# Issuing 72 spill stores from GpSimd's queue in place of SyncE's, in a two-layer hybrid backbone on one core

## The chip, the cores and the metric

The kernel runs on one core of a Trainium2 chip. The metric is the device time of one execution in microseconds; the median of three runs is taken. A core has four engines that compute (TensorE for matrix products, VectorE, ScalarE and GpSimd) and SyncE, which only issues transfers between the chip's main memory and the on-chip buffer. Each engine works through its own instructions in order, and an instruction that waits holds all that stand behind it on the same engine.

## What is computed

Two layers act on 512 latent tokens and 256 context tokens of width 1024. Each layer normalises its input, projects it to three groups of heads, and maps their gated outputs back:

```python
u = _modulate(h_lat, sh, sc) @ w_in[i]
y_hy = _hyena(u_hy, ...)                       # two long convolutions with implicit filters
xs, Bh, Ch, z_s, dt, a = _ssd_prep(u_ss, ...)
y_ss, _, _ = _ssd_bidir(xs, Bh, Ch, dt, a, s_f, s_b)   # chunked scan, both directions
y_ss = _ssd_finish(y_ss, xs, z_s, ...)         # gate and group norm
y_at = _window_attention(q, k, v, kc, vc, attn_sinks[i]) * jax.nn.silu(z_a)
out = jnp.concatenate([y_hy, y_ss, y_at], axis=-1) @ w_out[i]
new_lat = _layernorm(DEEPNORM_ALPHA * h_lat + g * out) * ln_g[i] + ln_b[i]
```

The context runs through the same weights; in the second layer only its keys, values and scan states are needed.

## The kernel before

Matrices stand in float32 and are split into a high and a low part, so that one product becomes three on TensorE. A projection (`proj`) loads a block of 128 x 1024 weights (L439), splits it (`split`, L178 on ScalarE and L179 on VectorE) and multiplies it with all tokens: 512 latent columns into the accumulator pl (two buffers, L461) and, where the context is needed, 256 columns into pc (one buffer, L463). The raw weight tile has two buffers, shared with the table loads of L202.

The on-chip buffer is too small for all that lies between the stages, so results are spilled to main memory and read back later. Five places store:

- `att` runs attention by blocks of 128 queries and stores each block's output (L686); the queries are read in through L611.
- `ssm` runs the scan by chunks of 128 tokens and stores each chunk's output (L863). Per chunk and group it loads a broadcast tile R (L844, three buffers) of row sums; VectorE and ScalarE add to it (L850, L852), and the product M of L857 is the last that reads it.
- `hy_in` projects the inputs of the long convolution, in steps V, 1, 2 and G, and stores each (L887 for V, L889 for the others). Step G reads step 2 back (L878).
- `gate_mul`, called by `ssm_gate` and `att_gate`, projects a gate, reads a spilled output back into U (L486), multiplies (L489) and stores it in place (L490). Its tile V has two buffers. Where the context is needed VectorE first clears the column between the sequences (L482), then forms the gate from the accumulators (L474).
- Other stores (of the filters, L349, of the long convolution's result, L991, and of the output) are not touched.

Between these, `modulation` loads weights through L365 and multiplies them (L370, then a copy L372 and L375); it is advanced one step at a time between projections. In the long convolution GpSimd takes one product of each frequency tile (L949), and in `ssm_gate` the power of the norm (L523).

All transfers are issued by SyncE before the change. Dependencies between tiles are tracked and turned into waits when the kernel is built, and a planner then lays out each engine's instructions; their order on an engine is not the order of the code. A load that reads a spilled tile back waits for the store to have landed, whichever queue issued it, and a buffer is reused only when the transfer that reads it has landed.

Of the kernel before, what the change touches and what calls it, by code (L numbers as in the profile page):

```python
# [18 lines left out]
P = 128  # L19
# [27 lines left out]
class Net:  # L47
# [428 lines left out]
    def gate_mul(self, l, b0, j, xt, sp, both):  # L476

        nc = self.nc
        n = WID if both else SEQ
        g = self.ip("V", [P, QW])  # L480
        if both:
            nc.vector.memset(g[:, SEQ:CO], 0.0)  # L482
        self.gate(*self.proj(l, b0 + j, xt, both), g)
        y = self.ip("U", [P, WID + 2])
        for c0, w in ((0, SEQ), (CO, CTX)) if both else ((0, SEQ),):
            nc.sync.dma_start(y[:, c0:c0 + w], sp[j, :, c0:c0 + w])  # L486
        if both:
            nc.vector.memset(y[:, SEQ:CO], 0.0)
        nc.vector.tensor_tensor(g[:, :n], y[:, :n], g[:, :n], op=ALU.mult)  # L489
        nc.sync.dma_start(sp[j, :, :n], g[:, :n])  # L490
        return g, y

    def att_gate(self, l, xt, sp, last):
# [97 lines left out]
    def att(self, l, q, ks, vt, last):  # L591

        nc = self.nc
        sp = self.dr.tile([4, P, QW], F32, name=self.nm("sp"))
        for n in list(range(4)) + ([] if last else [4, 5]):
            lat = n < 4
            q0 = n * P if lat else n * P + 1
# [67 lines left out]
            for hp in range(0, 4, 2):  # L665
                pts = []
                for i in range(nk):
# [4 lines left out]
                    t = self.w("pt", [P, 2, 256], bufs=5)  # L672
# [10 lines left out]
                        if i == 0:  # L683
                            self.after(m, turned)
            nc.scalar.activation(q[:, :, q0:q0 + P], pv.rearrange("p (h q) -> p h q", h=4), AF.Copy, scale=0.5)
            nc.sync.dma_start(sp[:, :, q0:q0 + P].rearrange("j p t -> p j t"), q[:, :, q0:q0 + P])  # L686
        return sp


# [90 lines left out]
    def ssm(self, l, xT, bt, bc, sc, rd, last):  # L780

        nc = self.nc
        sp = self.dr.tile([4, P, QW], F32, name=self.nm("sp"))
# [29 lines left out]
        for c in (0, 1, 2, 3) if last else (4, 5, 0, 1, 2, 3):  # L813
            q0 = col(c)
            pg = self.wk()
            for g in range(2):
                nc.tensor.matmul(pg[:, g * P:(g + 1) * P], lhsT=bc[:, g, q0:q0 + P], rhs=bc[:, 2 + g, q0:q0 + P], start=True, stop=True)
            gm = self.w("gm", [P, 2, P], bufs=2)
            nc.scalar.activation(gm, pg[:, 0:256].rearrange("p (g l) -> p g l", g=2), AF.Copy)

            own = self.ts([P, 10])
            for g in range(2):
                t = self.w("dg", [P, P])
                nc.vector.scalar_tensor_tensor(t, gm[:, g], 1.0, self.ident, op0=ALU.mult, op1=ALU.mult, accum_out=own[:, 8 + g:9 + g])
                w = slice(4 * g, 4 * g + 4)
                nc.vector.scalar_tensor_tensor(own[:, w], vec(DT, 1, c)[:, w], own[:, 8 + g:9 + g], dcol[:, w], op0=ALU.mult, op1=ALU.add)
            py = self.wk()
            ys = self.w("ys", [P, 512], bufs=3)
            nc.vector.tensor_tensor(h64(ys), h64(xT[:, c]), bc64(own[:, 0:8]), op=ALU.mult)
            for d in range(2):  # L830
                if states[d, c] is None:
                    continue
                po = self.wk()
                for g in range(2):
                    nc.tensor.matmul(po[:, 256 * g:256 * g + 256], lhsT=bc[:, 2 + g, q0:q0 + P], rhs=states[d, c][:, 256 * g:256 * g + 256], start=True, stop=True)
                yo = self.w("yo", [P, 512], bufs=3)
                nc.vector.tensor_tensor(h64(yo), h64(po), bc64(vec(EX, d, c)), op=ALU.mult)
                nc.vector.tensor_tensor(ys, ys, yo, op=ALU.add)
            for j in range(4):
                nc.tensor.matmul(py[:, j * P:(j + 1) * P], lhsT=ys[:, j * P:(j + 1) * P], rhs=self.ident, start=j == 0, stop=False, is_transpose=True, skip_group_check=True)  # L840

            for g in range(2):
                R = self.w("R", [P, 2, 4, P], bufs=3)
                nc.sync.dma_start(R, rd[:, 8 * c + 4 * g:8 * c + 4 * g + 4].partition_broadcast(P))  # L844
                for d in (1, 0):
                    for h in range(4):
                        hh = 4 * g + h
                        bias = vec(LB, d, c)[:, hh:hh + 1]
                        if h % 2 == 0 and d == 0:
                            nc.vector.tensor_scalar_add(R[:, d, h], R[:, d, h], bias)  # L850
                        else:
                            nc.scalar.activation(R[:, d, h], R[:, d, h], AF.Identity, bias=bias)  # L852
                E = R[:, 1]
                nc.vector.copy_predicated(E, self.upper.unsqueeze(1).to_broadcast([P, 4, P]), R[:, 0])
                nc.scalar.activation(E, E, AF.Exp)
                M = self.w("M", [P, 4, P], bufs=2)
                nc.vector.tensor_tensor(M, E, gm[:, g].unsqueeze(1).to_broadcast([P, 4, P]), op=ALU.mult)  # L857
                for h in range(4):
                    hh = 4 * g + h
                    r0, j = 64 * (hh % 2), hh // 2  # L860
                    nc.tensor.matmul(py[r0:r0 + 64, j * P:(j + 1) * P], lhsT=xT[:, c, 64 * hh:64 * hh + 64], rhs=M[:, h], start=False, stop=True, skip_group_check=True)
            nc.scalar.activation(bc[:, :, q0:q0 + P], py.rearrange("p (j l) -> p j l", j=4), AF.Copy, scale=0.5)
            nc.sync.dma_start(sp[:, :, q0:q0 + P].rearrange("j p t -> p j t"), bc[:, :, q0:q0 + P])  # L863
        return sp


    def hy_in(self, l, xt, last, b0, fill, x2s, sp, js=range(4)):
        nc = self.nc
        n = SEQ if last else WID
        for j in js:  # L870
            pl, pc = self.proj(l, b0 + j, xt, not last)
            t = self.ip("V", [P, QW])
            if b0 == B_GH:
                if not last:
                    nc.vector.memset(t[:, SEQ:CO], 0.0)
                self.gate(pl, pc, t)
                x2 = self.ip("U", [P, WID + 2])
                nc.sync.dma_start(x2[:, :n], x2s[j, :, :n])  # L878
                nc.vector.scalar_tensor_tensor(t[:, :n], t[:, :n], 0.5, x2[:, :n], op0=ALU.mult, op1=ALU.mult)
            else:  # L880
                i = C_HCW + 4 * ((b0 - B_HV) + j)
                self.conv(pl, pc, self.par[:, l, i:i + 4], t, False)
            if b0 == B_HV:

                f = self.ip("U", [P, WID + 2])
                for c0, L in ((0, SEQ),) if last else ((0, SEQ), (CO, CTX)):
                    nc.sync.dma_start(sp[j, :, c0:c0 + L], self.fold(t, f, c0, L))  # L887
            else:
                nc.sync.dma_start(sp[j, :, :n], t[:, :n])  # L889
            next(fill, None)  # L890

    def fold(self, v, f, c0, L):
# [476 lines left out]
```

## Time and profile before

| | us |
|---|---|
| median of 3 runs (1282.61 to 1287.61) | 1284.53 |
| the profiled execution | 1286.6 |
| its span, first to last instruction | 1284.8 |
| TensorE, busy in the span | 1212.7 |
| VectorE | 953.7 |
| ScalarE | 595.0 |
| GpSimd | 133.8 |

The transfers move 208.94 MB at a mean of 163 GB/s. TensorE's mean granted clock is 0.984 of full speed. A busy TensorE is not TensorE at its peak, since its products are pipelined and their ends are modelled; the idle time before an instruction, and what released it, say more. A wait for several things is put down to the one that came last.

### The profile page before, as it was taken

Reading aid. Unit: us, or ns where it says so; the run is one execution under the profiler, and the core shown is the slowest. Engines: PE = TensorE matmul, PEld = TensorE weight load, DVE = VectorE, ACT = ScalarE, POOL = GpSimd, SP = SyncE. Lnnn points to the kernel's source line nnn. Section 1 sums busy time; section 2 is a strip of 40 time slices with the busy share of each in tenths; the row PEclk is TensorE's granted clock in tenths of the full one; section 3 lists DMA queues with packets and bytes.
Section 4 is the critical chain, followed back from the end, with each engine's and each line's share of the span. In section 5 each row is a group of like instructions: output and inputs, shape, how many; then the busy total and the mean of one; then the engine's idle time right before and its main releaser. Section 6 shows DMA issues by size and latency. Waiting matters only on the chain.

```text
span 1284.8 us, 19311 instructions
## 1 busy us (share of the span) xinstructions
PE 1212.7 (94%) x6966; PEld 974.5 (76%) x6966; DVE 953.7 (74%) x1982; ACT 595.0 (46%) x1157; POOL 133.8 (10%) x117
## 2 busy tenths in 40 slices
PE   5988999999999999999999999999999999899997
PEld 3656788778776867799877777887877686788776
DVE  6986845987764885499746899777777588598676
ACT  5557623766434273333224454456644526343440
POOL 1421110000000000022110332100000000011102
PEclk9988999999999999999999999999999999999999
DMA  7775363321117477854488852431123725945872
GB/s 238 244 262 195 115 198 98 83 67 50 58 42 227 146 210 264 273 158 140 153 269 289 270 158 95 110 112 59 34 74 115 220 100 157 287 149 190 281 234 82
DMA packets 109192, 208.94 MB, mean 163 GB/s; under 512 B 10553, under 2 KB 55033, under 8 KB 109096
## 3 DMA queue, kind: packets, MB, share of 16 engines
q1 hardware_dynamic: 109096, 207.70, 51.3%
q8 instruction: 55, 0.90, 0.3%
q14 instruction: 41, 0.34, 0.1%
HBM read 162.44 MB, written 38.41 MB: 156 GB/s over the span
## 4 chain that ended last, share of the span: by engine, by line
PE 57%; DVE 14%; DMA 11%; issue 9%; ACT 4%; POOL 2%; SPq 1%; POOLq 0%; DVEq 0%; ACTq 0%
PE pl L461 19%; PE pc L463 7%; PE wk L183 4%; PE wk L184 4%; PE wk L185 4%; PE wk L682 3%; PE wk L671 3%; DMA R<-rd 2%; PE wk L633 2%; DVE wl L179 2%; PE wk L643 1%; PE wk L370 1%; DMA wo<-in_w_out_dram 1%; ACT wh L178 1%; DMA wr<-in_tab_dram 1%
## 5 line engine op out<-in xcount | busy, mean ns | idle before, releaser
L461 PE MATMUL pl<-Q,wh 128*128 128x512 f32 x1168 | 410.8, 403 | 0.9 <-ACT wh L178 0.5
L461 PEld LDWEIGHTS pl<-Q,wh 128*128 128x128 f32 x1168 | 218.1, 190 | 57.2 <-issue 8.1
L461 PE MATMUL pl<-Q,wl 128*128 128x512 f32 x584 | 233.0, 399 | 0.0
L463 PE MATMUL pc<-Q,wh 128*128 128x256 f32 x704 | 185.7, 291 | 6.0 <-DVE V L474 4.7
L178 ACT ACTIVATE wh<-wr 128x1024 fp32r<-128x1024 f32 x76 | 80.4, 1057 | 158.4 <-PE pc L463 76.8
L463 PEld LDWEIGHTS pc<-Q,wh 128*128 128x128 f32 x704 | 127.8, 191 | 13.7 <-DVE V L474 6.6
L461 PEld LDWEIGHTS pl<-Q,wl 128*128 128x128 f32 x584 | 110.8, 190 | 24.5 <-issue 1.2
L179 DVE TENSOR_TENSOR wl<-wr,wh 128x1024 fp32r<-128x1024 f32 x76 | 99.5, 1312 | 26.8 <-ACT wh L178 26.7
L949 POOL TENSOR_TENSOR ta<-ta 128x256 f32<-128x256 f32 x40 | 32.2, 804 | 712.3 <-DVE ta L947 687.0
L463 PE MATMUL pc<-Q,wl 128*128 128x256 f32 x352 | 101.7, 289 | 0.0
L463 PEld LDWEIGHTS pc<-Q,wl 128*128 128x128 f32 x352 | 67.2, 191 | 2.0 <-issue 1.4
L178 ACT ACTIVATE wh<-wo 128x1024 fp32r<-128x1024 f32 x30 | 31.6, 1058 | 47.0 <-DMA wo<-in_w_out_dram 27.1
L648 ACT ACTIVATE pr<-wk,S 128x512 f32<-128x512 f32 (+2 forms) x80 | 47.9, 604 | 11.5 <-DVE S L647 10.7
L852 ACT ACTIVATE R<-R,sc 128x128 f32<-128x128 f32 x120 | 38.4, 390 | 26.3 <-DMA R<-rd 26.3
L646 DVE TENSOR_REDUCE S<-wk 128x1 f32<-128x512 f32 (+2 forms) x80 | 45.0, 578 | 6.9 <-PE wk L644 4.1
L179 DVE TENSOR_TENSOR wl<-wo,wh 128x1024 fp32r<-128x1024 f32 x30 | 36.5, 1221 | 12.5 <-ACT wh L178 12.4
L671 PE MATMUL wk<-con,pr 128*128 128x128 f32 x320 | 45.4, 277 | 0.1
L183 PE MATMUL wk<-ph,Q 128*128 128x256 f32 x144 | 41.7, 298 | 2.8 <-ACT ph L178 2.7
L671 PEld LDWEIGHTS wk<-con,pr 128*128 128x128 f32 x320 | 36.1, 140 | 8.4 <-issue 4.4
L178 ACT ACTIVATE yh<-ta 128x512 fp32r<-128x512 f32 x32 | 20.2, 631 | 47.3 <-DVE ta L950 47.3
L184 PE MATMUL wk<-plo,Q 128*128 128x256 f32 x144 | 41.3, 291 | 0.3 <-DVE plo L179 0.3
L185 PE MATMUL wk<-ph,Q 128*128 128x256 f32 x144 | 40.6, 288 | 0.0
(404 smaller groups left out, 2901.1 us busy)
## 6 DMA issues: line engine op xcount, KB each, us to landing
wr<-in_w_in_dram SPq DMA_DIRECT2D x76, 512.0 KB, 4.3
Q<-in_w_mod_dram SPq DMA_DIRECT2D x24, 1024.0 KB, 8.0
wo<-in_w_out_dram SPq DMA_DIRECT2D x43, 512.0 KB, 5.0
kd<-k SPq DMA_DIRECT2D x40, 256.0 KB, 2.3
R<-rd SPq DMA_DIRECT2D x20, 512.0 KB, 6.1
kt<-kd SPq DMA_DIRECT2D x40, 256.0 KB, 3.0
sp<-V SPq DMA_DIRECT2D x20, 384.5 KB, 3.8
cs<-sp SPq DMA_DIRECT2D x60, 128.0 KB, 4.8
```

Of the source, the lines that this page charges most:

```text
L178: nc.scalar.activation(hi, src, AF.Copy)
L179: (nc.gpsimd if lo_on == "p" else nc.vector).tensor_tensor(lo, src, hi.bitcast(F32), op=ALU.subtract)
L183: mm(out, lhsT=lh, rhs=rh, start=start, stop=False, **k)
L184: mm(out, lhsT=lh, rhs=rl, start=False, stop=False, **k)
L185: mm(out, lhsT=ll, rhs=rh, start=False, stop=stop, **k)
L461: nc.tensor.matmul(pl, lhsT=w[:, k * P:(k + 1) * P], rhs=x[:, 0:SEQ], start=s, stop=e)
L463: nc.tensor.matmul(pc[:, 0:CTX], lhsT=w[:, k * P:(k + 1) * P], rhs=x[:, SEQ:SEQ + CTX], start=s, stop=e)
L646: nc.vector.tensor_reduce(m[:, h:h + 1], sa[:, :ws], axis=AX.X, op=ALU.max)
L648: nc.scalar.activation(pr[:, h, :ws], sa[:, :ws], AF.Exp, bias=negm[:, h:h + 1], scale=0.125, accum_out=sums[:, h:h + 1])
L671: turned = nc.tensor.transpose(ps[:, (2 * g + h) * P:(2 * g + h + 1) * P], prs[g][:, hp + h, i * P:(i + 1) * P], self.ident)
L682: m = nc.tensor.matmul(pv[r0:r0 + 64, hp * P:hp * P + 256], lhsT=vt[:, keys[i], r0:r0 + 64], rhs=pts[i][:, g], start=i == 0 and hp == 0, s ...
L852: nc.scalar.activation(R[:, d, h], R[:, d, h], AF.Identity, bias=bias)
```

## The change

The five kinds of store are issued from GpSimd's queue; all loads and the other stores stay on SyncE's.

```diff
@@ gate_mul
         nc.vector.tensor_tensor(g[:, :n], y[:, :n], g[:, :n], op=ALU.mult)
-        nc.sync.dma_start(sp[j, :, :n], g[:, :n])
+        nc.gpsimd.dma_start(sp[j, :, :n], g[:, :n])
         return g, y
@@ att
             nc.scalar.activation(q[:, :, q0:q0 + P], pv.rearrange("p (h q) -> p h q", h=4), AF.Copy, scale=0.5)
-            nc.sync.dma_start(sp[:, :, q0:q0 + P].rearrange("j p t -> p j t"), q[:, :, q0:q0 + P])
+            nc.gpsimd.dma_start(sp[:, :, q0:q0 + P].rearrange("j p t -> p j t"), q[:, :, q0:q0 + P])
@@ ssm
             nc.scalar.activation(bc[:, :, q0:q0 + P], py.rearrange("p (j l) -> p j l", j=4), AF.Copy, scale=0.5)
-            nc.sync.dma_start(sp[:, :, q0:q0 + P].rearrange("j p t -> p j t"), bc[:, :, q0:q0 + P])
+            nc.gpsimd.dma_start(sp[:, :, q0:q0 + P].rearrange("j p t -> p j t"), bc[:, :, q0:q0 + P])
@@ hy_in
                 for c0, L in ((0, SEQ),) if last else ((0, SEQ), (CO, CTX)):
-                    nc.sync.dma_start(sp[j, :, c0:c0 + L], self.fold(t, f, c0, L))
+                    nc.gpsimd.dma_start(sp[j, :, c0:c0 + L], self.fold(t, f, c0, L))
             else:
-                nc.sync.dma_start(sp[j, :, :n], t[:, :n])
+                nc.gpsimd.dma_start(sp[j, :, :n], t[:, :n])
```

## Rows read from the trace of the kernel before

**Rows 1.** The page, part 1: busy us (share of the span), instructions.
```profile
PE 1212.7 (94%) x6966; PEld 974.5 (76%) x6966; DVE 953.7 (74%) x1982; ACT 595.0 (46%) x1157; POOL 133.8 (10%) x117
```
**Rows 2.** TensorE in order of time: start, us, instruction [idle before <-releaser], four stretches.
```profile
407.98 1.34 PE L375 MATMUL wk<-U,sel 128*4 128x512 f32 x2 [2.28 <-DVE U L372]
...
452.44 0.78 PE L835 MATMUL wk<-st,Q 128*128 128x256 f32 x2 [2.31 <-ACT gm L819]
...
536.47 0.62 PE L183 MATMUL wk<-ph,Q 128*128 128x256 f32 x3 [2.71 <-ACT ph L178]
...
643.39 0.39 PE L463 MATMUL pc<-Q,wh 128*128 128x256 f32 x1 [1.79 <-DVE V L474]
```
**Rows 3.** Waits of TensorE, whole span: us in total, times, longest.
```profile
PE pc L463 <- DVE V L474: 4.7, 3, 1.9
...
PE wk L370 <- DMA Q<-in_w_mod_dram: 2.9, 1, 2.9
```
**Rows 4.** Waits of SyncE's queue, whole span, at three of the stores.
```profile
SPq L686 <- ACT Q L685: 67.4, 10, 16.9
...
SPq L889 <- DVE V L540: 45.6, 13, 13.8
...
SPq L490 <- DVE V L489: 23.4, 11, 3.3
```
**Rows 5.** SyncE's queue in order of time, 394 to 398 us.
```profile
394.03 0.37 SPq L365 DMA_DIRECT2D Q<-in_w_mod_dram  x1
397.42 0.34 SPq L889 DMA_DIRECT2D sp<-V  x1
397.80 0.43 SPq L844 DMA_DIRECT2D R<-rd  x1
```
**Rows 6.** The chain that ended last, at 440 us: start, us, what.
```profile
439.58 0.60 DVE M L857
```
**Rows 7.** SyncE's queue in order of time, 442 to 443 us.
```profile
442.14 0.37 SPq L863 DMA_DIRECT2D sp<-Q  x1
442.60 0.46 SPq L844 DMA_DIRECT2D R<-rd  x1
```
**Rows 8.** SyncE's queue in order of time, 525 to 528 us.
```profile
525.35 0.32 SPq L878 DMA_DIRECT2D U<-sp  x1
526.87 0.32 SPq L889 DMA_DIRECT2D sp<-V  x1
527.28 0.39 SPq L202 DMA_DIRECT2D wr<-in_tab_dram  x1
```
**Rows 9.** SyncE's queue in order of time, 996 to 999 us.
```profile
996.02 0.34 SPq L439 DMA_DIRECT2D wr<-in_w_in_dram  x1
998.46 0.32 SPq L887 DMA_DIRECT2D sp<-U  x1
998.88 0.38 SPq L365 DMA_DIRECT2D Q<-in_w_mod_dram  x1
```
**Rows 10.** Waits of VectorE, whole span, at L482.
```profile
DVE V L482 <- DMA sp<-V: 17.2, 4, 6.8
```
**Rows 11.** VectorE in order of time, in the gate stage of layer 0.
```profile
634.76 0.96 DVE L489 TENSOR_TENSOR V<-U,V 128x769 f32<-128x769 f32 x1 [0.41 <-DMA U<-sp]
...
642.31 0.06 DVE L482 MEMSET V<- 128x1 f32 x1 [3.36 <-DMA sp<-V]
```
**Rows 12.** SyncE's queue in order of time, at 637 us.
```profile
637.02 0.32 SPq L490 DMA_DIRECT2D sp<-V  x1
```
**Rows 13.** GpSimd's groups: form, count | busy us, mean ns | idle before, releasers.
```profile
L949 POOL TENSOR_TENSOR ta<-ta 128x256 f32<-128x256 f32 x40 | 32.2, 804 | 712.3 <-DVE ta L947 687.0 <-ACT yh L178 23.7 <-ACT th L473 1.6
```
**Rows 14.** GpSimd in order of time, 728 to 766 us.
```profile
728.14 2.40 POOL L1110 TENSOR_TENSOR hn<-hn,lgb 128x1024 f32<-128x1024 f32 x1
...
758.94 6.59 POOL L1110 TENSOR_TENSOR hn<-hn,lgb 128x1024 f32<-128x1024 f32 x1 [3.09 <-DVE hn L1109]
```
**Rows 15.** SyncE's queue in order of time, at 21 us.
```profile
21.48 0.42 SPq L716 DMA_DIRECT2D dw<-in_w_dt_dram  x1
```

## The prediction, made before the changed kernel ran

> **What bounds the kernel now.** I read the page's busy times first. TensorE is busy 1212.7 us of a span of 1284.8 [rows 1], so it is idle for 72.1 us, and whatever a changed queue can give back lies inside those. GpSimd is busy 133.8 us [rows 1]: it has room for more instructions, though not necessarily at the moment they come. Next I read TensorE's instructions in order of time for idle stretches, and for each one asked what released it. Work of several stages is interleaved on TensorE, so most waits elsewhere are covered by a projection; the idle stretches that stand are short and can be counted.
>
> Then the waits of SyncE's queue, where all stores and loads stand in one line. The stores that the change moves hold it often: 67.4 us in ten waits at L686, 45.6 us in thirteen at L889, 23.4 us in eleven at L490 [rows 4]. That total is no gain by itself. A hold costs time only where the load behind it was ready and TensorE later ran dry for it. The largest, L686, closes a block of attention; no idle stretch of TensorE that I found in that stage follows it, so I value it at nothing. What covers it is the projections laid between the blocks; without that cover a single hold could cost up to its length, at most 16.9 us [rows 4].
>
> Four places pass the test.
> (a) SyncE issued a load at 394.03 that took 0.37 to issue, then waited for a store of L889 until 397.42, and issued the third load of R at 397.80 [rows 5]. The two loads of R before it had gone out, so its source was written, and its pool has three buffers: it was ready, and lost 397.80 - 394.40 = 3.4 us. VectorE, in order behind R, reached the copy L372 late, and TensorE idled 2.28 us for it [rows 2]. Recoverable: the smaller, 2.28.
> (b) R's buffer was freed by the product M of L857, which ended at 439.58 + 0.60 = 440.18 [rows 6]; the load went out at 442.60, right behind a store of L863 at 442.14 [rows 7]. Lost 2.42; TensorE idled 2.31 at the state product L835, which waited for ScalarE, itself in order behind R [rows 2]. Recoverable 2.31.
> (c) A table load at 527.28 stands right behind a store of L889 at 526.87; the issue before ended at 525.35 + 0.32 = 525.67 [rows 8]. Held at most 1.61, before an idle stretch of 2.71 at the first transforms [rows 2].
> (d) A load of modulation weights at 998.88 stands behind a store of L887 at 998.46; the issue before ended at 996.02 + 0.34 = 996.36 [rows 9]. Held at most 2.52, and TensorE waited 2.9 us for that tile [rows 3].
> All together 2.28 + 2.31 + 1.61 + 2.52 = 8.7 us. In (a) and (b) the load's readiness is seen; in (c) and (d) it is not, and the load's own buffer may have come free late, so I take half: 4.6 + 2.1 = **6.7 us gained**.
>
> **The change part by part.** It moves 72 store issues: 16 of L490, 10 of L686, 10 of L863, 12 of L887, 24 of L889. What is computed and what is transferred stay the same.
>
> Taken from SyncE: the issue, 0.32 us for the stores of [rows 8, 9, 12], and the hold before it. Issue time alone is worth nothing, since SyncE has idle time around each.
>
> Put on GpSimd: no row of this kernel shows GpSimd issuing a transfer. From below, the price on its queue is SyncE's 0.32 us [rows 12], or less than nothing where the store leaves a busy line. From above, the longest GpSimd instruction here, 6.59 us for one that took 2.40 us 31 us earlier [rows 14]: its work is stretched when VectorE is busy. I take 0.80 us, the mean of the 40 instructions of L949 [rows 13], the ordinary price of a short step on this engine, and call it X; it also delays the landing by as much.
>
> Where a late landing hurts: the gate multiplication. VectorE clears one column of the next buffer V at L482 before it runs the gate's product L474 of the current one, and the buffer is free only when its store has landed. VectorE waited 17.2 us in four such waits [rows 10], one of them 3.36 us long up to 642.31 [rows 11], and TensorE, whose one small accumulator pc is read by L474, idled 4.7 us in three [rows 3], 1.79 of it there [rows 2]. So X falls on the end three times: 3 x 0.80 = 2.4. Against it stands the first of those stores: its product ended at 634.76 + 0.96 = 635.72 [rows 11], but SyncE issued it at 637.02 [rows 12], so 1.3 us of hold go. Net **1.1 us lost**. The stores of the two projection stages use the same two buffers but have a whole projection between them, so 0.8 us later costs nothing there; if that cover is gone it is 0.8 us for each.
>
> What is queued behind a store on GpSimd: in attention, scan and the projections nothing that is due soon. In the gate stage the power L523, and where the planner lays gates among the long convolution, the products L949, for which VectorE and then TensorE wait. I count four stores among them (an estimate), 4 x 0.80, half of it passed on: **1.6 us lost**. The loads that read a store back come a stage later, except in the last gates before the output projection, whose tiles are taken last in its order, so they lose nothing.
>
> Sum: 6.7 - 1.1 - 1.6 = 4.0 us gained. Against the profiled execution, 1286.6 us around a span of 1284.8, that gives 1282.6; the median of the runs, 1284.5, lies 2.1 below that execution, so I say **1280.5 us**. An unknown remains: the order of instructions is not the code's but a planner's at build time, as the load of dw shows, which the code places in the scan's preparation and which SyncE issues at 21.48 us [rows 15]. Another queue for 72 instructions can re-deal orders elsewhere. No row prices that; I allow it the size of the four gains, 8.7 us, either way in the range.
>
> What a rule of the skill says here: the longest row of GpSimd shows a stretch by 6.59 - 2.40 = 4.2 us [rows 14]. The Trainium skill (SBUF — State Buffer, "SBUF: two separate sides") says that GpSimd writes the descriptors of its own transfers through a port that it shares with VectorE, that some VectorE operations lock it out, and that a transfer of about 620 ns then took about 3100. By that difference, 2.5 us, as X, an estimate from that page, the sum would be 6.7 - (7.5 - 1.3) - 5.0 = 4.5 us lost, 1289.0. No run shown so far has such a transfer; VectorE stood idle in the wait of [rows 11], which speaks for the smaller price.
>
> **The rivals.**
> *All of it comes through.* All four holds go in full (8.7) and the stores in the gate stage no longer queue behind loads, so that its 4.7 us of idle time [rows 3] go too: 13.4 us, 1271.1. For it: SyncE held the store at 637.02 behind other issues. Against it: the landing itself, 642.3 less 637.0, is most of that wait, and it is a transfer of bytes, which stays.
> *Stores land late (slower).* GpSimd's issue is stretched as in [rows 14], X = 4.2, in all four waits at L482: 4 x 4.2 - 1.3 = 15.5 lost, less 6.7: 8.8 slower, 1293.3; with X = 6.59 about 18 slower. It turns the sign of the whole from 4X - 1.3 = 6.7, X = 2.0 on. For it: the four waits have no slack. Against it: VectorE is mostly idle there, since it is itself waiting.
> *GpSimd is held instead.* The wait of 23.4 us at L490 [rows 4] moves to GpSimd, with L949 behind it for a quarter of the stores: 5.9, and 3.2 for the issues, in place of 1.6: 6.7 - 1.1 - 9.1, so 3.5 slower, 1288.0.
> *Nothing comes loose.* Each load's own wait ends where the store's did, or a load before it holds it as long: no gain, 1.1 + 1.6 lost, 1287.2. The Trainium skill (DMA: Bandwidth & Descriptors, "Issuing engines are not separate DMA queues") speaks for it: issuing from more engines saves only the issue time. The holds of [rows 5, 7] speak against it: a held line is more than issue time.
>
> **How the numbers follow.** Chances: my forecast 0.31, all of it 0.27, late landing 0.20, GpSimd held 0.10, nothing loose 0.12. The range takes the forecast with 8.7 us below it and, above, the late landing with some of its tail: 1268 to 1300. About 0.5%, 6.4 us, is what a measurement of this kernel can tell from no change. Faster by more than that (under 1278.1): all of the second case and a third of the forecast's spread, 0.37. Slower (over 1290.9): the late landing, a part of GpSimd held, 0.25. The rest, 0.38, within.
>
> **What would show it.** Right: the idle stretches at the counterparts of 407.98 and 452.44 shrink to under 1 us, the loads of R leave SyncE without a store's wait, the waits at L482 stay near 17 us in sum. GpSimd's issues near 0.8 us each would confirm X; 2 us or more, or waits at L482 over 25 us, would mean the slower rival. L949 waiting for GpSimd's own queue would mean the third. It is wrong altogether if TensorE's order comes out different in whole stages, which would show as idle stretches where before had none.

## The result, and the profile after

The changed kernel takes 1303.75 us (median of six runs, 1299.02 to 1306.32), the kernel before 1284.84 in the same comparison: a ratio of 1.0132, 95% interval 1.0106 to 1.0158. By the ratio it is slower by 17 us. The profiled execution took 1306.32 us, its span is 1304.5.

The page, part 1 (busy us, share of the span, instructions), and the row that part 3 has for the new queue (packets, MB, share of the transfer engines' time):

```profile
PE 1215.2 (93%) x6966; PEld 977.2 (75%) x6966; DVE 952.3 (73%) x1982; ACT 593.9 (46%) x1157; POOL 175.4 (13%) x189
...
q0 software_dynamic: 5632, 20.99, 4.4%
```

TensorE is as busy as in [rows 1], 1215.2 us against 1212.7, but idle for 1304.5 - 1215.2 = 89.3 us in place of 72.1. So 17.2 of the 19.7 us by which the span grew are idle time of TensorE. Where it lies is read from TensorE's instructions in order of time (start, us, instruction, idle before and its releaser):

```profile
405.69 0.39 PE L463 MATMUL pc<-Q,wh 128*128 128x256 f32 x1 [0.48 <-DVE U L536]
...
449.81 1.13 PE L835 MATMUL wk<-st,Q 128*128 128x256 f32 x4 [1.57 <-ACT gm L819]
...
458.93 0.66 PE L861 MATMUL wk<-M,Q 128*64 128x128 f32 x8 [1.40 <-DVE M L857]
...
528.93 0.80 PE L463 MATMUL pc<-Q,wh 128*128 128x256 f32 x2 [4.00 <-DVE V L474]
...
672.97 0.80 PE L463 MATMUL pc<-Q,wh 128*128 128x256 f32 x2 [6.76 <-DVE V L474]
...
1122.42 0.80 PE L183 MATMUL wk<-ph,Q 128*128 128x256 f32 x2 [6.72 <-ACT ph L178]
...
1221.04 1.22 PE L461 MATMUL pl<-Q,wh 128*128 128x512 f32 x2 [5.69 <-DVE V L474]
```

The stretches of [rows 2] at 407.98 and 452.44 have shrunk from 2.28 and 2.31 to 0.48 and 1.57. Against that stand long ones where before had short ones or none: 4.00, 6.76, 6.72 and 5.69, 23 us together. The waits say the same. TensorE's for the gate product, 4.7 us in [rows 3], is 12.9 on pc. The group on pl is new, and the one for ph, which before is the single 2.71 of [rows 2], is 6.7. VectorE's at L482 is what it was, 17.2 us in [rows 10]:

```profile
PE pc L463 <- DVE V L474: 12.9, 4, 6.8
PE pl L461 <- DVE V L474: 6.7, 2, 5.7
PE wk L183 <- ACT ph L178: 6.7, 1, 6.7
...
DVE V L482 <- DMA sp<-V: 17.5, 4, 5.2
```

GpSimd's own groups (busy us, mean ns of one | idle before) show a cheap issue, 0.54 to 0.56 us for the stores L889 and L490 of one row per partition, 0.76 for attention's, of four pieces per partition:

```profile
L889 POOL DMA_DIRECT2D sp<-V x24 | 13.1, 544 | 213.3 <-DVE V L540 81.6 <-DVE sc L771 57.2 <-DVE V L879 42.2
L490 POOL DMA_DIRECT2D sp<-V x16 | 8.9, 557 | 88.9 <-DVE V L489 83.3 <-DVE U L488 5.6
L686 POOL DMA_DIRECT2D sp<-Q x10 | 7.6, 763 | 185.9 <-ACT Q L685 185.9
```

The longest of the 72 took 0.83 us. So the price on the queue is not where the time went; the order of instructions is the next thing to read. Printed engine by engine, the order of the changed kernel differs from that of before on every engine, TensorE included, although no line but the five stores was touched. On GpSimd one pair of old instructions has changed places: in both layers the addition L1003, which waits for a load of gg, now stands ahead of the second power L523. The end of layer 1's gates shows what that does, all engines in order of time, first after, then before:

```profile
1203.65 0.32 SPq L486 DMA_DIRECT2D U<-sp  x1
1204.40 0.17 DVE L522 TENSOR_SCALAR S<-S 128x4 f32<-128x4 f32 x1
...
1207.37 2.40 POOL L1003 TENSOR_TENSOR gg<-gg,hr 128x1024 f32<-128x1024 f32 x1 [4.95 <-DMA gg<-gd]
1209.73 1.53 POOL L523 TENSOR_TENSOR S<-S,mhalf 128x4 f32<-128x4 f32 x1
...
1211.28 0.32 SPq L524 DMA_DIRECT2D rsd<-S  x1
1211.70 0.37 SPq L486 DMA_DIRECT2D U<-sp  x1
1212.17 0.38 SPq L1056 DMA_DIRECT2D cs<-sp  x1
...
1217.25 0.48 DVE L1059 SCALAR_TENSOR_TENSOR cs<-cs,par,rb 128x256 f32<-128x256 f32 x1 [6.88 <-DMA cs<-sp]
```

```profile
1190.55 0.17 DVE L522 TENSOR_SCALAR S<-S 128x4 f32<-128x4 f32 x1
1190.80 1.01 POOL L523 TENSOR_TENSOR S<-S,mhalf 128x4 f32<-128x4 f32 x1 [11.10 <-DVE S L522]
1191.84 0.32 SPq L524 DMA_DIRECT2D rsd<-S  x1
```

Before, L523 starts 0.08 us after L522 ends, and SyncE stores its result at once. After, L522 ends at 1204.57, L523 starts at 1209.73, and SyncE, in order behind the small store L524, issues nothing from 1203.97 to 1211.28. The loads of U and cs leave only behind it, VectorE waits 6.88 us, TensorE then 5.69.

### The profile page after: what moved, and what is told of

Same layout as the page of the kernel before. It is cut to its first block, busy times and chain, and to the rows that moved or that the text cites. A ratio compares the mean times of both kernels' runs of the same rounds, so it can differ in the third digit from the quotient of the medians.

```text
span 1304.5 us, 19389 instructions
## 1 busy us (share of the span) xinstructions
PE 1215.2 (93%) x6966; PEld 977.2 (75%) x6966; DVE 952.3 (73%) x1982; ACT 593.9 (46%) x1157; POOL 175.4 (13%) x189
## 4 chain that ended last, share of the span: by engine, by line
issue 44%; PE 27%; DMA 11%; DVE 10%; POOL 4%; ACT 3%; SPq 1%; POOLq 0%; DVEq 0%; ACTq 0%
PE pl L461 7%; PE wk L183 4%; PE wk L184 4%; PE wk L185 3%; PE pc L463 3%; DMA wr<-in_tab_dram 2%; DMA wo<-in_w_out_dram 2%; DMA gg<-gd 1%; DVE wl L179 1%; DMA sp<-V 1%; DVE S L398 1%; DMA wr<-in_w_in_dram 1%; DMA cs<-sp 1%; PE pc L370 1%; DVE hn L1096 1%
## 5 line engine op out<-in xcount | busy, mean ns | idle before, releaser
L463 PE MATMUL pc<-Q,wh 128*128 128x256 f32 x704 | 187.5, 294 | 14.7 <-DVE V L474 12.9
L178 ACT ACTIVATE wh<-wr 128x1024 fp32r<-128x1024 f32 x76 | 80.4, 1058 | 158.0 <-PE pc L463 71.6
L463 PEld LDWEIGHTS pc<-Q,wh 128*128 128x128 f32 x704 | 128.9, 194 | 23.0 <-DVE V L474 15.6
L463 PE MATMUL pc<-Q,wl 128*128 128x256 f32 x352 | 102.4, 291 | 0.0
L463 PEld LDWEIGHTS pc<-Q,wl 128*128 128x128 f32 x352 | 68.0, 193 | 2.0 <-issue 1.4
L178 ACT ACTIVATE wh<-wo 128x1024 fp32r<-128x1024 f32 x30 | 31.6, 1056 | 38.5 <-DMA wo<-in_w_out_dram 17.9
L178 ACT ACTIVATE yh<-ta 128x512 fp32r<-128x512 f32 x32 | 20.0, 630 | 58.5 <-DVE ta L950 58.3
L183 PE MATMUL wk<-ph,Q 128*128 128x256 f32 x144 | 40.4, 295 | 6.7 <-ACT ph L178 6.7
L949 POOL TENSOR_TENSOR ta<-ta 128x256 f32<-128x256 f32 x40 | 31.6, 791 | 106.1 <-DVE ta L947 82.8
L179 DVE TENSOR_TENSOR wl<-wo,wh 128x1024 fp32r<-128x1024 f32 x30 | 38.6, 1290 | 9.2 <-ACT wh L178 9.1
L889 POOL DMA_DIRECT2D sp<-V x24 | 13.1, 544 | 213.3 <-DVE V L540 81.6
L178 ACT ACTIVATE cx<-cs 128x256 fp32r<-128x256 f32 x54 | 21.3, 407 | 43.3 <-DVE cs L1059 30.4
```

The source lines that it names most:

```text
L178: nc.scalar.activation(hi, src, AF.Copy)
L179: (nc.gpsimd if lo_on == "p" else nc.vector).tensor_tensor(lo, src, hi.bitcast(F32), op=ALU.subtract)
L183: mm(out, lhsT=lh, rhs=rh, start=start, stop=False, **k)
L463: nc.tensor.matmul(pc[:, 0:CTX], lhsT=w[:, k * P:(k + 1) * P], rhs=x[:, SEQ:SEQ + CTX], start=s, stop=e)
L949: nc.gpsimd.tensor_tensor(ta[:, 0], ta[:, 0], ta[:, 1], op=ALU.subtract)
```

## The experiments

Three theories stood at first. **A**: that swap on GpSimd costs the time. **B**: stores land later, since loads that SyncE used to hold behind them now run beside them. **C**, formed on the way: the planner's re-dealt order as a whole costs it, not the queue. All runs in one table. The stage columns are worked out: the median time of TensorE's instructions against the same instructions in the profile of before, as the change from one place to the next (places in us of before). Up to 600, gate_only and queue_gate run the code of before, and their first columns read -4.3, 0.9 and -2.5, -0.3. So an entry is good to some 2 us, up to 440 worse. A ratio sets a kernel against runs of the kernel before from the same comparison, and is not the quotient of two medians, so rows are compared by ratios. A stage column is read from one execution, and that need not be a typical one: the profiled run of queue_no_gate was the slowest of its twelve (1289.22), so its columns add up to a loss that its ratio does not show, and the changed kernel's was the slowest of its six.

| run | median | ratio to before (95%) | to 440 | 440-600 | 600-720 | 720-1070 | 1070-1185 | 1185-1236 |
|---|---|---|---|---|---|---|---|---|
| changed kernel | 1303.75 | 1.0132 (1.0106-1.0158) | -1.9 | 4.3 | 5.9 | 2.7 | 2.8 | 7.4 |
| gp_order | 1300.78 | 1.0111 (1.0083-1.0139) | -3.5 | 5.8 | 4.0 | 4.6 | 3.9 | 0.0 |
| gp_order_rsd | 1300.73 | 1.0112 (1.0084-1.0139) | -5.6 | 5.2 | 4.8 | 1.8 | 4.9 | 2.3 |
| no_gate | 1289.88 | 1.0036 (1.0009-1.0063) | -2.9 | 4.8 | -4.9 | 4.8 | 4.6 | 0.8 |
| gate_only | 1295.26 | 1.0057 (1.0032-1.0082) | -4.3 | 0.9 | 5.7 | 6.7 | -1.0 | 1.4 |
| queue_only | 1285.56 | 0.9989 (0.9973-1.0004) | -3.6 | 2.6 | 2.4 | -1.5 | 0.0 | -0.2 |
| order_only | 1313.18 | 1.0195 (1.0168-1.0222) | -1.3 | 12.5 | 6.7 | 5.5 | 3.3 | 6.6 |
| queue_no_gate | 1282.07 | 0.9956 (0.9935-0.9977) | -1.9 | 3.3 | 1.1 | 2.1 | -0.3 | -0.3 |
| queue_gate | 1289.66 | 1.0030 (1.0008-1.0053) | -2.5 | -0.3 | 3.5 | 3.5 | -1.7 | -0.2 |
| fix_act | 1301.83 | 1.0115 (1.0071-1.0158) | -3.8 | 4.6 | 5.0 | 1.2 | 2.0 | 6.7 |
| fix_gate | 1308.06 | 1.0164 (1.0122-1.0206) | -4.4 | 4.4 | 10.6 | 2.5 | 2.6 | 2.2 |
| fix_both | 1303.22 | 1.0110 (1.0067-1.0153) | -2.4 | 7.5 | 10.1 | 4.7 | 2.2 | 0.5 |
| fix_gate_2 | 1300.16 | 1.0093 (1.0062-1.0124) | -2.9 | 5.5 | 1.4 | 2.5 | 4.0 | 2.2 |
| fix_both_2 | 1296.46 | 1.0071 (1.0049-1.0093) | -4.8 | 6.3 | 1.2 | 2.7 | 0.5 | 2.2 |
| inject_l1 | 1290.25 | 1.0026 (1.0002-1.0049) | -3.7 | 1.5 | 3.9 | -1.9 | 0.0 | 4.0 |
| queue_late_add | 1289.03 | 1.0014 (0.9991-1.0037) | -4.9 | 0.1 | 4.3 | -0.5 | -1.0 | 1.5 |
| queue_first_add | 1283.29 | 0.9968 (0.9949-0.9988) | -2.5 | 1.5 | 2.4 | 0.6 | 1.1 | -0.3 |

### One swap put back, and one small store moved

gp_order adds one order edge to the changed kernel; gp_order_rsd also moves the store L524.

```diff
@@ ssm_gate
-            nc.gpsimd.tensor_tensor(mc[:, 1, :nch], mc[:, 0, :nch], self.mhalf[:, :nch], op=ALU.pow)
+            self.pw = nc.gpsimd.tensor_tensor(mc[:, 1, :nch], mc[:, 0, :nch], self.mhalf[:, :nch], op=ALU.pow)
@@ out, gate
-            nc.gpsimd.tensor_tensor(g, g, bm, op=ALU.add)
+            add = nc.gpsimd.tensor_tensor(g, g, bm, op=ALU.add); self.after(add, self.pw)
```

> The changed kernel with one thing put back: on GpSimd the power L523 of the second group stands ahead of the gate's addition L1003 again, as it did before the change, in both layers. All 72 stores stay on GpSimd, and no other engine's order differs from the changed kernel's. Theory A (the addition, which waits for the load of gg, delays L523, so SyncE stands at the small store L524 with the loads of U and cs behind it): TensorE's idle stretches of 6.76 us at 666 and 5.69 us at 1215 shrink by half or more, L524 leaves SyncE within 2 us of L522's end, and the time falls by 7 to 12 us, to 1292 to 1297. Theory B (the stores land later among loads that nothing holds back): the loads of U go out earlier but the waits at L482 stay near 17 us, and the time falls by 3 us at most, to 1301 or more.

> As the kernel with L523 put back ahead of L1003, and the four small stores L524 of the norm's factor are issued by GpSimd too, right behind the power that they wait for, so that SyncE never stands for it. Theory A: as fast as the kernel with the order put back or up to 2 us faster, 1291 to 1297, since SyncE's loads of U have no wait for GpSimd left. Theory B: no change against the kernel with the order put back, 1301 or more.

In gp_order every other engine's order stayed that of the changed kernel, but for one split of VectorE near 545; in gp_order_rsd VectorE's, ScalarE's and SyncE's were dealt anew, so it is not a test of one thing. In layer 1 of gp_order A holds to the letter: the column 1185-1236 falls from 7.4 to 0.0, and L524 leaves 1.1 us after L522's end. In layer 0 it does not: 5.9 became 4.0. The trace of gp_order, layer 0, tells why:

```profile
651.44 0.51 DVE L521 TENSOR_REDUCE S<-U 128x6 f32<-128x192 f32 x1
654.11 0.17 DVE L522 TENSOR_SCALAR S<-S 128x6 f32<-128x6 f32 x1 [2.15 <-issue]
654.13 0.06 DVE L482 MEMSET V<- 128x1 f32 x1
654.36 2.28 POOL L523 TENSOR_TENSOR S<-S,mhalf 128x6 f32<-128x6 f32 x1 [5.26 <-DVE U L488]
...
656.67 0.32 SPq L524 DMA_DIRECT2D rsd<-S  x1
...
660.57 0.96 DVE L489 TENSOR_TENSOR V<-U,V 128x769 f32<-128x769 f32 x1 [4.20 <-DMA U<-sp]
```

In the re-dealt order of VectorE the clearing L482 stands ahead of L522 (the printed order shows it; in the trace the two start within 0.02 us). It waits for the store of the gate just multiplied, issued at 648.56 and landed at 654.08. So a landing holds the norm, the norm holds L524, and L524 holds SyncE. In gp_order_rsd this chain is gone: L522 starts at 651.17 without a wait, and four loads of U leave from 650.21 on. Yet the column reads 4.8, and TensorE idles 3.10, 1.42, 1.25 and 2.75 us before products on pc where before has 1.79, 1.95 and 0.99. What costs that is not shown.

The whole gained 0.2%, within the intervals of both, and 1300.8 is about what B expected (1301 or more), whose loads of U, though, waited as A said. By the columns A is one cause (inject_l1, below, tests it alone), not the cause.

### Which stores

no_gate puts the 16 stores L490 back on SyncE, gate_only moves these alone; the planner is free in both.

```diff
@@ gate_mul (no_gate)
-        nc.gpsimd.dma_start(sp[j, :, :n], g[:, :n])
+        nc.sync.dma_start(sp[j, :, :n], g[:, :n])
```

> The changed kernel with the 16 stores of the gated outputs (L490) back on SyncE; the other 56 stay on GpSimd. L523 stands ahead of L1003 on GpSimd again, and the order of SyncE in the gate stage is nearly that of before. Theory A and theory B both put the loss of the gate stages (6.5 + 7.7 us) down to these 16 stores, so both expect 1288 to 1292; what is left above the 1284.8 of before is then the re-dealt order of the stages ahead (520 to 540, about 3 us, and 1100, about 1 us), less the 3.1 us won at 400. If the time stays over 1297, the loss lies with the other 56 stores, and both theories fall.

> The kernel before with only the 16 stores of the gated outputs (L490) on GpSimd. In layer 0 the planner puts L1003 ahead of the second L523, in layer 1 it does not. Theory A: a loss in layer 0 alone, about 5 us, 1288 to 1291, and no idle stretch over 3 us at the end of layer 1's gates. Theory B: a loss in both layers, 10 to 15 us, 1295 to 1300.

no_gate fell where both theories put it, with the stretch at the first transforms of layer 1 hardly changed (6.14 us), which neither had foreseen. gate_only lost in layer 0's gates and behind them and nearly nothing in layer 1's, as A said, but 7 us by its ratio in place of 5; B's 10 to 15 us did not come. In both the planner dealt the order anew, so they can't part queue from order.

### The queue without the order, and the order without the queue

For that the order itself was tied: each engine's instructions chained by order edges (no waits) to the order of another kernel. Stores on GpSimd, and in order_only the moved stores on SyncE, are not in these chains: the planner places them among the rest.

```diff
@@ end of tile_backbone_kernel
+    ins = {i.name: i for i in tc.nc.all_instructions()}
+    for names in chains:
+        for x, y in zip(names, names[1:]):
+            tc.add_manual_dep(ins[y], x, no_sync, reason="order")
```

> All 72 stores on GpSimd as in the changed kernel, but the order of instructions on TensorE, VectorE, ScalarE, and of SyncE's loads and GpSimd's arithmetic, is tied to the order of the kernel before. So only the queue changes. Theory C (the loss is the planner's re-dealt order: L1003 ahead of L523, the clearing L482 ahead of L522 on VectorE, two more table copies L203 ahead of the first transforms' L178 on ScalarE at 1113): all of the loss goes and the gains of the prediction are left, 1277 to 1286, with no idle stretch of 6 us at the first transforms of layer 1. Theory B (the stores, no longer ahead of loads that SyncE holds back, land late): the loss stays wherever a store frees a buffer, 1292 to 1300.

> The kernel before with all stores on SyncE, but with the order of instructions on TensorE, VectorE, ScalarE, GpSimd and of SyncE's loads tied to that of the changed kernel; the planner puts the stores among SyncE's loads. So only the order changes. Theory C: slow, 1294 to 1306, with idle stretches of 5 us and more where the changed kernel has them (666, 1115, 1215). Theory B: as fast as before within 0.5%, 1279 to 1291.

> The order of the kernel before kept on all engines, with the 56 stores of attention, scan and convolution inputs on GpSimd and the 16 gated outputs on SyncE in their old places. Theory C: 1276 to 1282, the gains of the prediction's (a) to (d) without any price in the gate stage. Theory B: about 1284, since convolution inputs that land late take back the gains.

> The order of the kernel before kept on all engines, with only the 16 gated outputs (L490) on GpSimd. Theory C: 1283 to 1288, the price of 16 issues from another queue, 0.27 us later each, at four waits. Theory B: the loss of the gate stages stays, 1290 to 1296.

These four settle the main question. All 72 stores on GpSimd in the old order: 0.9989, no change that can be told; the same queue in the new order, the changed kernel: 1.0132. **The loss is the order's.** (The old queue in the new order, 1.0195, shows the sign but not the size: it is slower than the changed kernel itself, since the planner had to put the stores into a line laid out without them, or for another reason; that is not shown.) B falls as the cause of the loss: in queue_only the four gate stores whose landing VectorE awaits take 6.2, 5.5, 5.9 and 5.2 us from issue to landing; in before the three that its waits at L482 show took 5.3, 6.9 and 6.1, the first in [rows 11, 12].

The queue alone then splits. 56 stores without the gates gain 0.44%, about 5.7 us; the 16 gate stores alone lose 0.30%, about 3.9; the median of queue_gate, 1289.66, lies between C's 1283 to 1288 and B's 1290 to 1296. queue_no_gate beats both kernels and is the version to keep. Why the gate stores lose shows in queue_only, layer 0:

```profile
656.34 2.40 POOL L1003 TENSOR_TENSOR gg<-gg,hr 128x1024 f32<-128x1024 f32 x1 [7.70 <-DMA gg<-gd]
658.67 0.60 POOL L490 DMA_DIRECT2D sp<-V  x1
...
664.66 0.06 DVE L482 MEMSET V<- 128x1 f32 x1 [10.09 <-DMA sp<-V]
...
666.95 0.80 PE L463 MATMUL pc<-Q,wh 128*128 128x256 f32 x2 [5.45 <-DVE V L474]
```

The product of that store had ended at 654.45, and GpSimd issued it 4.23 us later, because L1003 ahead of it waited for its load until 656.34. On SyncE the store had nothing of GpSimd's ahead of it. L482 waited 10.09 us, TensorE 5.45 where no such wait of [rows 3] is over 1.9 us.

### Where L1003 stands

The old order tied, only L1003 of layer 0 moved on GpSimd (in queue_late_add that of layer 1 too).

```diff
@@ chain of GpSimd (queue_late_add)
-L1003, L490, L490, L490, L490
+L490, L490, L490, L490, L1003
@@ chain of GpSimd (queue_first_add)
-L1003, L490, L490, L490, L490
+L490, L1003, L490, L490, L490
```

> The order of the kernel before tied on all engines, all 72 stores on GpSimd, and on GpSimd the addition L1003, which waits for the load of gg, behind the last gate store of its layer. Theory C: the store that stood 4.23 us behind L1003 at 654 goes at once, the wait of 10.1 us at L482 falls to 6, and TensorE's idle 5.45 us at 667 to 2: 3 to 4 us under the kernel with the order of before alone, 1280 to 1283 beside 1286 for before, a ratio of 0.995 to 0.997. Rival D (the store's landing among loads sets the wait): no change, a ratio of 0.998 to 1.000.

> The order of the kernel before tied on all engines, all stores on GpSimd, and in layer 0 L1003 stands right behind the first gate store of attention, so neither does the store wait for it nor is its buffer hr held. Theory C: that store goes at once, TensorE's idle 5.5 us at 667 falls to about 3, no stall at 691: 2 to 4 us under queue_only, a ratio of 0.996 to 0.998. Rival E: as queue_only, 0.999 or more.

Behind all gate stores, the first stall shrank as expected (L482 10.09 to 7.33, TensorE 5.45 to 2.96), and another came: L1003 also reads a buffer of hr, whose next load L1090 held SyncE's line for 11.24 us at 671.56, and TensorE idled 2.64 us at 691.66 for a weight behind it. No gain in sum. Behind the first store alone the store goes at once, TensorE's stretch is 3.73, nothing new appears, and the ratio is 0.9968 (0.9949 to 0.9988). It overlaps queue_only's, so a gain by this move is not shown. Nor is the wait at L482 gone: it is 9.02 us, since this store, issued at 655.03, lands only at 663.82, after 8.8 us where queue_only's took 5.9. Here a late landing, B's mechanism, took back most of what the earlier issue gave.

### Putting places of the order back, and putting one in

fix_act, fix_gate and their sums tie the changed kernel's own order, with a few places as before. The one on ScalarE is read here in layer 1, after and then before: table copies L203, each waiting for its load, stand ahead of the first splits ph (L178), and TensorE waits 6.72 us for those.

```profile
1113.71 0.63 ACT L203 ACTIVATE Q<-wr 128x512 fp32r<-128x512 f32 x1 [2.90 <-DMA wr<-in_tab_dram]
1115.76 1.06 ACT L203 ACTIVATE Q<-wr 128x1024 fp32r<-128x1024 f32 x1 [1.42 <-DMA wr<-in_tab_dram]
1120.34 1.06 ACT L203 ACTIVATE Q<-wr 128x1024 fp32r<-128x1024 f32 x1 [3.52 <-DMA wr<-in_tab_dram]
1121.31 0.58 ACT L473 ACTIVATE th<-pl 128x512 f32<-128x512 f32 x1
1121.78 1.07 ACT L178 ACTIVATE ph<-wk 128x512 fp32r<-128x512 f32 x2
```

```profile
1102.06 1.58 ACT L203 ACTIVATE Q<-wr 128x1024 fp32r<-128x1024 f32 x2 [4.67 <-DMA wr<-in_tab_dram]
1103.55 0.58 ACT L473 ACTIVATE th<-pl 128x512 f32<-128x512 f32 x1
1105.76 1.24 ACT L178 ACTIVATE ph<-wk 128x512 fp32r<-128x512 f32 x2 [1.64 <-PE wk L929]
```

```diff
@@ chain of ScalarE, layer 1 (fix_act, fix_both, fix_both_2)
-L203, L203, L203, L473, L178 ph, L178 ph, L203
+L203, L473, L178 ph, L178 ph, L203, L203, L203
@@ chain of VectorE, layer 0 (fix_gate, fix_both and their second forms)
-L521, L482, L522
+L521, L522, L482
@@ chain of GpSimd, layer 0 (fix_gate, fix_both)
-L1003, L523, L490, L490, L490, L490
+L523, L490, L490, L490, L490, L1003
@@ chain of GpSimd, layer 0 (fix_gate_2, fix_both_2)
-L1003, L523, L490, L490, L490, L490
+L523, L490, L1003, L490, L490, L490
```

Not shown: in layer 0 copies L203 on ScalarE change places with L473 in the same way. In layer 1 L1003, which stands ahead of L523 in the changed kernel, goes behind the last gate store in fix_gate and fix_both, and right behind L523, as before the change, in the second forms.

> The changed kernel with its own order tied on all engines, but for one thing on ScalarE: the table copies L203 that it places ahead of the last gate activations L473 (layer 0) and of the first splits L178 of the long convolution (layer 1) stand behind them again, as before the change. Theory C (these re-dealt places cost the time): the idle stretches of 4.0 us at 529 and 6.7 us at 1122 shrink under 2 us, 4 to 8 us gained on the changed kernel's 1304, so 1296 to 1300. Rival D (the stall only moves, since the tables' products wait for the same copies): 1301 or more.

> The changed kernel with its own order tied on all engines, but for two things in the gate stages: on GpSimd the addition L1003 stands behind the last of the layer's gate stores, and on VectorE the clearing L482 that waits for a store stands behind the norm's L522, not ahead of it. Theory C: L523 and the small store L524 follow at once, the loads of U leave SyncE in time, and the idle stretches of 6.8 us at 673 and 5.7 us at 1215 go to 2 us or less: 9 to 14 us gained, 1290 to 1295. Rival D: layer 0's stretch stays since its gate stores land 6 to 7 us after their issue: as the kernel with only L523 put back, 1298 to 1301.

> Both sets of places put back, all 72 stores on GpSimd, the rest of the changed kernel's order kept. Theory C: the sum of the two, 13 to 20 us gained, 1284 to 1291. Rival D: 1296 or more.

All three missed. fix_act's two stages hardly moved: in layer 0 the stall came back a little later (1.57 us at 532.01 for the weight split wh, then 1.45 at 534.20 for ph), and in layer 1 the 6.72 us before ph fell to 0.62, but 4.34 us came up at 1121.91 before the products of yh, so 0.8 us went, less than one profile can tell. That is what D said. fix_gate made the stage slower, and its trace shows that the repair, not the theory, was at fault:

```profile
671.28 20.84 SPq L1090 DMA_DIRECT2D hr<-in_ctx_dram  x2
...
689.14 2.62 POOL L1003 TENSOR_TENSOR gg<-gg,hr 128x1024 f32<-128x1024 f32 x1
...
700.09 0.79 PE L183 MATMUL wk<-wh,cx 128*128 128x512 f32 x1 [4.55 <-ACT wh L178]
```

Moved behind the last gate store, L1003 freed hr at 691.8 and held SyncE for 20.8 us, as in queue_late_add. The second forms put it where it holds neither:

> The changed kernel with its own order tied on all engines, but for the gate stages: on GpSimd L1003 stands behind L523 again in both layers (in layer 0 also behind the first gate store of attention), and on VectorE the clearing L482 stands behind L522. Theory C (these places cost the gate stages' loss): TensorE's idle at 673 falls from 6.8 to about 3, at 1215 from 5.7 to under 1, no new stall near 700, 8 to 12 us gained: 1292 to 1296, a ratio of 1.004 to 1.008. Rival E (the loss is spread over the whole re-dealt order, and what is put back at one place returns at the next): 1300 or more, a ratio of 1.010 or more.

> As fix_gate_2, with the table copies L203 on ScalarE put back too. Theory C: 1 to 3 us less than fix_gate_2. Rival E: the same as the changed kernel within 0.3%.

Layer 0's gates fall from 5.9 to 1.4 and 1.2, layer 1's from 7.4 to 2.2, and with the copies back the transforms of layer 1 from 2.8 to 0.5. fix_gate_2's ratio, 1.0093, lies between C and its rival, its median, 1300.16, in the rival's range: it settles nothing alone; fix_both_2, 1.0071 (1.0049 to 1.0093), is clear of the changed kernel's 1.0106 and gained 0.61%, 7.8 us. So these places are worth about half of the 17 us. Not all of it is order put back: behind the first gate store L1003 stands in a place that it did not have before the change either, and what that alone gives (0.2% in queue_first_add) could not be told from nothing.

The reverse test puts the swap of layer 1 alone into the good order of queue_only.

```diff
@@ chain of GpSimd, layer 1
-L523, L1003
+L1003, L523
```

> The order of the kernel before tied on all engines, all stores on GpSimd, with one swap put in: in layer 1 the addition L1003 stands ahead of the power L523 on GpSimd, as in the changed kernel. Theory C: L523 waits for the load of gg, L524 and SyncE's loads behind it leave 4 us and more later, and TensorE idles 4 to 6 us near 1210: 4 to 8 us over the 1285.6 of queue_only, a ratio of 1.002 to 1.006. Rival E: no change, a ratio of 0.997 to 1.001.

The ratio went from 0.9989 to 1.0026, by 4.8 us, as C said; the chain is the one of the changed kernel, L522 at 1190.25, then:

```profile
1192.77 2.39 POOL L1003 TENSOR_TENSOR gg<-gg,hr 128x1024 f32<-128x1024 f32 x1 [4.49 <-DMA gg<-gd]
1195.12 1.03 POOL L523 TENSOR_TENSOR S<-S,mhalf 128x4 f32<-128x4 f32 x1
1196.17 0.33 SPq L524 DMA_DIRECT2D rsd<-S  x1
```

The single idle stretch of 4 to 6 us that was expected did not appear; the stage's 4.0 us came in stretches under 1 us each.

**What stays open:** the other half. Between 440 and 600 the changed kernel's order costs 4 to 8 us in every variant with the stores on GpSimd, and none of the places put back helped. Set against queue_only, which has the same queue and the old order, fix_both_2 loses 6.3 - 2.6 = 3.7 us there and as much, 2.7 + 1.5 = 4.2, between 720 and 1070; each is a difference of two single executions. Late landings may have a part: the four gate stores that took 6.2, 5.5, 5.9 and 5.2 us to land in queue_only take 7.0, 7.2, 6.6 and 6.2 in the changed kernel. No run parts that from the order, and none mixes the old order of the loads with the new one of the arithmetic.

## Why the prediction was wrong

The prediction said 1280.5 us in a range of 1268 to 1300; 1303.75 lies above the range. (By its own words, the forecast less 8.7 us, the range would begin at 1271.8; that has no bearing here.) Step by step:

**The four gains.** (a) came through: the third load of R leaves at 395.71 right behind the load at 395.29, the copy L375 does not wait, and in place of 2.28 us [rows 2] 0.48 are left before its neighbour L463. The stage shortened by more, 3.1 us, but 2.0 and 2.3 of that show up in gate_only and queue_gate too, whose code up to there is that of before; that part was the execution's, not the change's (its clock, see the last section). (b) half: 2.31 became 1.57, and the product M then ended last twice more, 1.40 (at 458.93) and 1.30 us (at 477.51); the stage as a whole gained nothing. That is the case the prediction asks of every stall, what is late next, and it did not ask it here. (c) nothing: with the order kept, 3.36 us in queue_only where [rows 2] has 2.71. (d) came through with the order kept (no idle time before L370 at 1007.59 in queue_only, 2.9 in [rows 3]), but in the changed kernel 2.34 us of it stand at 1015.25.

**X.** Taken at 0.80 us; 0.54 to 0.76 was measured, and a store issues 0.30 us behind its product where SyncE took 0.03. The waits at L482 stayed at 17.5 us, so the rival of late landing (X = 4.2, over 25 us) is out. One of the four waits at L482 was misread, though:

```profile
530.86 0.06 DVE L482 MEMSET V<- 128x1 f32 x1 [3.89 <-DMA sp<-V]
```

It waits for the store of L889 at 526.87 [rows 8], not for a gate store: in the projections too a store that lands late can hold VectorE, where the prediction put nothing. In queue_only this wait is 6.08 us.

The Trainium skill (SBUF — State Buffer, "SBUF: two separate sides"), by which the prediction weighed an X of 2.5 us, has GpSimd kept from writing its descriptors while some VectorE operations run; no issue of these 72 took over 0.83 us, so no run here shows it.

**What stands around a store on GpSimd.** The prediction counted what is queued behind the stores, L949 and L523, 1.6 us. It did not look for what stands ahead of them. In the trace of before L1003 is GpSimd's next instruction behind the second L523 and starts at 660.58, while the first of the last four gate stores left SyncE at 656.77: on one queue, behind L1003, it had to wait.

```profile
656.77 0.32 SPq L490 DMA_DIRECT2D sp<-V  x1
660.58 2.41 POOL L1003 TENSOR_TENSOR gg<-gg,hr 128x1024 f32<-128x1024 f32 x1 [9.40 <-PE pc L463]
```

The gate stage's price was 1.1 + 1.6 = 2.7 us forecast, about 3.9 us measured (queue_gate). This was one mechanism of it, 4.23 us in one place; with L1003 moved 0.9989 became 0.9968, which the intervals do not part. The rival "GpSimd is held" had the right resource and the wrong holder.

**The sum with the order kept.** 4.0 us forecast, 0.9989 measured, 1.4 us with an interval from 3.5 gained to 0.5 lost. The terms differ more than the sum: the 56 stores gained 5.7 (6.7 forecast), the gates lost 3.9 (2.7 forecast). The Trainium skill (DMA: Bandwidth & Descriptors, "Issuing engines are not separate DMA queues") would have had nothing but issue time to gain. The issue time of 56 stores is 56 x 0.32 = 18 us on SyncE, so 5.7 us gained do not contradict that by their size. What does is (a): of the 3.4 us that a ready load lost, 0.34 were issue time, the rest a place in the line.

**The step that failed** is the last one, the planner. The prediction saw that "another queue for 72 instructions can re-deal orders elsewhere", had no row for its price, and gave it the size of the four gains, 8.7 us, either way, without a chance of its own. It measured 1.0132 / 0.9989, 1.4% or 18 us, one way only. It even named the sign, "idle stretches where before had none", and that is what the trace shows at 528.93, 1122.42 and 1221.04. A re-dealt order should have been a rival with its own place and price. One place could have been named: if L523, due when L522 ends, must wait for a load on GpSimd, SyncE stands at L524 with the loads of U behind it. The price only a run gave: 4.8 us for layer 1 alone (inject_l1).

## What to carry to other kernels

When a planner orders the instructions, moving an issue to another queue is two changes, the queue and a new deal of every engine's order; tie the old order before you judge the queue (here 0.9989 against 1.0132). Before a store goes to a computing engine's queue, look for the instruction ahead of it there that waits for a load, and for every buffer that this instruction frees. A place that is put back proves itself only if the next holder, a buffer or a queue, is read too: much the same repair gave 1.0164 with L1003 behind the last gate store of each layer, and 1.0093 with it behind the first in layer 0 and behind L523 in layer 1.

## What the runs showed of the hardware

An idle stretch of TensorE can cost more than its length. Busy time by stretches (us, busy time of each engine, granted clock, share of the transfer engines, GB/s) in the kernel before, then in the changed one:

```profile
395.00:440.00 45.00, 42.72 (x224) 32.97 (x223) 30.50 (x60) 14.40 (x31) 0.00 (x0) 0.96 0.48 151
660.00:680.00 20.00, 17.06 (x96) 14.32 (x95) 9.29 (x19) 5.31 (x10) 2.41 (x1) 1.00 0.84 272
```

```profile
395.00:440.00 45.00, 44.52 (x255) 34.45 (x251) 33.66 (x64) 17.01 (x34) 1.63 (x3) 1.00 0.54 180
660.00:680.00 20.00, 13.24 (x61) 11.42 (x60) 7.37 (x16) 3.36 (x7) 1.14 (x2) 0.74 0.84 256
```

Over 20 us around the idle 6.76 us the granted clock averaged 0.74, so for part of them TensorE had the lower of its levels, 1.2 in place of 2.4 GHz. Part of that fell into the idle time and cost nothing; over the 7.03 us from its end, 672.97, to 680, TensorE was busy throughout at a mean clock of 0.58: (1 - 0.58) x 7.03 = 3.0 us of work lost.

The kernel before has the same in small. In the 10 us behind each of the four idle stretches of [rows 2] (2.28, 2.31, 2.71 and 1.79 us) the granted clock averaged 0.83, so some (1 - 0.83) x 10 = 1.7 us of work went with each, beyond the stretch itself. The prediction, which took TensorE's idle time for all that there is to give back, left that out. But a stall is not always followed by it: behind the idle 2.9 us of [rows 3], which ended at 1007.67, the clock stayed at 1.00 for the next 10 us, as it did around the 1.50 us of (a) in queue_gate. So at (a) the kernel before lost (1 - 0.96) x 45 = 1.8 us by the clock, and gate_only and queue_gate, with 1.80 and 1.50 us of idle time there, lost none.

Over the whole span the mean clock was 0.984 in the kernel before and 0.979 in the changed one, (0.984 - 0.979) x 1300 = 6.5 us, some of it in idle time; between the profiles it ran from 0.974 (order_only) to 0.987 (queue_late_add), 17 us. That may be one reason why single profiles of the same code differ by 2 us at one place.

At their shortest, transfers land alike from either queue: L889's took 2.3 us from issue to landing on both, L887's 2.4 from SyncE and 2.1 from GpSimd. The median of L889 went from 3.5 to 3.8 us and its longest from 4.9 to 7.3; why is not shown. Of the 24 stores of L889 before the change the trace shows only 7 landings.
